# The transfers of the weight sums of a Strassen-like product: all from GpSimd, and mostly beside the first MLP product

## The chip, the core and the metric

One core of a Trainium2 chip runs the whole kernel. The metric is device time in microseconds of one execution. The engines are TensorE (PE in the profile; its weight loads are PEld), VectorE (DVE), ScalarE (ACT), GpSimd (POOL) and SyncE (SP, which only issues transfers). Transfers run on 16 DMA engines; SP, ACT and POOL each have a queue of their own to issue them from, which in the profile are q1 (SP), q10 (ACT) and q0 (POOL).

## What is computed

One layer of an encoder, on 512 tokens and 16 learned ones ahead of them, with 1024 channels, in float32:

```
h = concatenate([meta, x])
u = rmsnorm(h); proj = u @ w_in
y_rw = rwkv7_branch(...)      # a recurrence over the tokens, 8 heads
y_fx = fox_branch(...)        # attention with a forget gate, 8 heads
merged = gateA * (y_rw @ w_out_rw) + gateB * (y_fx @ w_out_fx)
h = h + merged @ w_o
z = rmsnorm(h)
h = h + square(relu(z @ w_up)) @ w_down
```

w_up is 1024 x 4096, w_down 4096 x 1024. The change is about the last line only.

## The kernel before, in words

**Split products.** Large products run on pairs of reduced-precision factors: each weight tile of 128 x 512 is loaded by SP into a buffer `wraw`, ScalarE makes its high part `whi` (a cast), VectorE or GpSimd its low part `wlo` (the difference), and TensorE does three matmuls for each product: high by high, high by low, low by high (`passes`). `load_h` (L230 to 238) does this for one tile, `load_w` for two; `wraw`, `whi` and `wlo` have four buffers each. In the front the same is done by `convert` (L442), with the low part on GpSimd (L450).

**Stages.** The front computes the projections of u, the recurrence and the attention together. Streams of work (Python generators) are woven into one another by `Turns.run` (L166), which follows a planned TensorE time, the `Clock`: a stream yields the planned time from which it may go on, and has a rank. TensorE's order is written out by it; the other engines' instructions are ordered by priority. Gate projections leave through `gt` (L489), which uses the buffers of `wraw`. Then comes the merge (L1055 to 1133): output projections with gates, where GpSimd adds the two branches (L1070), w_o, and the second norm. Then comes the MLP.

**The MLP.** Its hidden dimension is done in three slices of 4, 6 and 6 pairs of blocks (`SLICES`). In each slice the first product, w_up, is computed (L1145, 24 matmuls of 512 columns for a block of 128 hidden channels), two blocks to a pair. `up_evac` (L1148) squares what is positive into R; after the second block of a pair `left_factors` (L1154) makes seven left factors of R. R has two buffers, taken in turn. Then the second product, w_down, runs (L1235) as seven products on quarters in place of eight (Winograd's form of Strassen's scheme): (A11, B11), (A12, B21), (A22, T4), (S2, T2), (S3, T3), (S1, T1), (S4, B22), in this order. Each uses n_pairs right tiles, one for each pair, with six matmuls to a tile; `fill` (L1174) calls `load_h` for the next right tile, two tiles ahead before the product begins.

**The weight sums.** T1 to T4 are sums of quarters of w_down and are made by the DMA engines, from HBM to HBM: T1 = B11 + B12, T3 = B12 + B22, T2 = B22 + T1, T4 = B21 + T2. Each quarter is cut into eight parts c of 256 x 512 (512 KB), and each sum of each part takes a copy and then an accumulating transfer: 64 steps. Right tile j of a slice comes from part c = j // 2, so slice 0 needs c = 0 and 1, slice 1 needs 2 to 4, slice 2 needs 5 to 7. In before, `weight_sums` (L1002) is a stream of rank -1 in the front: step n waits for planned time 45 + 6 n us. Copies are issued by ScalarE (L1024), additions by GpSimd (L1022), each tied behind the last instruction of its engine that was written out until then; a copy stands about three steps ahead of its addition. The sums are loaded in the MLP by L233.

Of the kernel before, what the change touches and what calls it, by code (L numbers as in the profile page):

```python
# [9 lines left out]
F32 = mybir.dt.float32  # L10
# [4 lines left out]
ALU = mybir.AluOpType  # L15
# [12 lines left out]
CDEC = math.exp(-0.5)  # L28
SLICES = (4, 6, 6)
FIRST = (0, 4, 10)  # L30


C_MU = 0
# [155 lines left out]
def kernel(ctx, tc, ht, x, win, par, cst, gain, lora, wout, wo, wup, wdn, out, dbg=None):  # L189
    nc = tc.nc  # L190
# [3 lines left out]
    V, G, A = nc.vector, nc.gpsimd, nc.scalar  # L194
# [72 lines left out]
    gates_d = [dr.tile([128, S], F32, name=f"gd{i}") for i in range(16)]  # L267
    quarters = [[wdn[i][256 * c:256 * c + 256] for c in range(8)] for i in range(4)]
    tsum = [[dr.tile([256, 512], F32, name=f"tsum{i}") for c in range(8)] for i in range(4)]

    with ExitStack() as st:
        up = st.enter_context(tc.tile_pool(name="up", bufs=1))
# [49 lines left out]
        with tc.tile_pool(name="xp", bufs=2) as xp:  # L322
# [14 lines left out]
            for t in range(2):  # L337
# [13 lines left out]
                n = 0  # L351
# [303 lines left out]
        class Pair:  # L655
            def __init__(self, p):
                self.p, self.b0 = p, B_PAIR + 6 * p + 3
# [341 lines left out]
        turns.add(2, attention())  # L999
        turns.add(3, fox_features())  # L1000
        def weight_sums():

            def part(t, c):
                return t[c].rearrange("(a b) c -> a (b c)", b=2)

            def behind(dma, engine):
                x = next(x for x in reversed(nc.cur_bb.bb.instructions) if str(x.engine).endswith(engine) and x.name != dma.ins.name)
                tc.add_manual_dep(dma.ins, x.name, mybir.DependencyInfo(mybir.DependencyClass.NoSync, mybir.DependencyReason.DATA),
                                  reason="spread over the front")

            t1, t2, t3, t4 = tsum
            b11, b12, b22, b21 = quarters
            steps = []
            for c in range(8):
                for a, b in (((t1, b11), (t1, b12)), ((t3, b12), (t3, b22)), ((t2, b22), (t2, t1)), ((t4, b21), (t4, t2))):
                    steps += [(*a, c, False), (*b, c, True)]
            for n in range(1, len(steps) - 2, 2):
                steps[n], steps[n + 1] = steps[n + 1], steps[n]
            for n, (dst, src, c, adds) in enumerate(steps):
                yield lambda: 45.0 + 6.0 * n  # L1020
                if adds:
                    behind(nc.gpsimd.dma_start(part(dst, c), part(src, c), accum_op=ALU.add, max_dma_last_dim=2048), "Pool")  # L1022
                else:
                    behind(nc.scalar.dma_start(part(dst, c), part(src, c), max_dma_last_dim=2048), "Activation")  # L1024

        turns.add(-1, weight_sums())
        turns.add(8, projections(24 + 16))
# [20 lines left out]
    with ExitStack() as st:  # L1048
# [6 lines left out]
        for m in range(KB):  # L1055
            w = load_w(wout[m])
            pp = []
            for br in range(2):
# [4 lines left out]
                n = 0  # L1063
# [46 lines left out]
        for i in range(4):  # L1110
            po = ppo()
            n = 0
# [25 lines left out]
    with ExitStack() as st:  # L1138
        dp = st.enter_context(tc.tile_pool(name="dp", bufs=1))
# [8 lines left out]
        def up_evac(po, out):  # L1148

            r = dp.tile([128, 512], F32, name="r", bufs=2)  # L1150
            act(r, po, AF.Relu)
            V.scalar_tensor_tensor(out, po.rearrange("p (a b) -> p a b", b=256), 0.0, r.rearrange("p (a b) -> p a b", b=256), ALU.max, ALU.mult)

        def left_factors(fhi, flo, j, R):  # L1154

            def halves(a, b):
                A.copy(fhi[:, j, a:b], R[:, a:b])  # L1157
                V.tensor_tensor(flo[:, j, a:b], R[:, a:b], fhi[:, j, a:b].bitcast(F32), ALU.subtract)  # L1158

            halves(0, 3)  # L1160
            a11, a12, s1, s2, s4 = (R[:, i, :] for i in (A11, A12, S1, S2, S4))
            V.tensor_tensor(R[:, S3:S1 + 1, :], R[:, 0:3:2, :], bc(R[:, 7, :], 1, 2), ALU.subtract)
            V.tensor_tensor(s2, a11, s1, ALU.add)
            V.tensor_tensor(s4, s2, a12, ALU.subtract)  # L1164
            halves(3, 7)
# [20 lines left out]
        def soon(*jobs):  # L1186
            later.extend(jobs)

        for p0, n_pairs in zip(FIRST, SLICES):
            fhi = dp.tile([128, max(SLICES), 7, 256], F32R, name="fhi")  # L1190
            flo = dp.tile([128, max(SLICES), 7, 256], F32R, name="flo")
            blocks = list(range(2 * p0, 2 * (p0 + n_pairs)))
            held, R = [], None
            if p0 == 0:

                ws, pos = early + [load_w(wup[2])], [ppo() for i in range(3)]
                for w, po in zip(ws, pos):
                    up_part(w, po, 0, 256)
                held = list(zip(ws, pos))
            for n, b_ in enumerate(blocks):  # L1200
                if held:
                    w, po = held.pop(0)
                    up_part(w, po, 256, 512)
                else:
                    w = load_w(wup[b_])
                    po = ppo()
                    up_part(w, po, 0, 512)
                if n == 2 * n_pairs - 1:
                    fill(AHEAD)
                if n % 2 == 0:  # L1210
                    R = yp.tile([128, 8, 256], F32, name="R", tag=("y_rw", "y_fx")[n // 2 % 2])
                    up_evac(po, R[:, 0:8:7, :])
                else:
                    up_evac(po, R[:, 1:3, :])
                    left_factors(fhi, flo, n // 2, R)

            first, last = p0 == 0, p0 + n_pairs == 16

            def product(x, left, start, stop, end=False):

                for j in range(n_pairs):
                    fill(1)
                    w = ready.pop(0)
                    if later:
                        later.pop(0)()
                    if end and j >= n_pairs - 2:
                        if j == n_pairs - 2:
                            held = w
                            continue
                        order = [(i, j + d, (held, w)[d + 1]) for i in range(2) for d in (-1, 0)]  # L1230
                    else:
                        order = [(i, j, w) for i in range(2)]
                    for i, k, u in order:
                        for n, (a, c) in enumerate(passes((fhi, flo), u)):
                            mm(x[i], a[:, k, left, 128 * i:128 * i + 128], c, start=start and k == 0 and n == 0,  # L1235
                               stop=stop and k == n_pairs - 1 and n == 2)

            def own(left, end=False):
                x = [ppo() for i in range(2)]
                product(x, left, True, True, end)  # L1240
                return x

            def gathered(v, left):
                for i, x in enumerate(own(left)):
                    if first:
                        A.copy(v[:, i], x)
                    else:
                        V.tensor_tensor(v[:, i], v[:, i], x, ALU.add)

            def add(a, b, i, x, op):  # L1250
                h = hr[a][b][:, i]
                V.tensor_tensor(h, h, x, op)

            def store(a, b, i):
                r0 = 256 * a + 128 * i
                nc.sync.dma_start(out[r0:r0 + 128, 512 * b:512 * b + 512], hr[a][b][:, i])

            def added(a, b, left, op, end=False):
                for i, x in enumerate(own(left, end)):
                    add(a, b, i, x, op)  # L1260
                    if end:
                        store(a, b, i)

            gathered(v1, A11)
            added(0, 0, A12, ALU.add)
            if last:
                for i in range(2):
                    soon(lambda i=i: (add(0, 0, i, v1[:, i], ALU.add), store(0, 0, i)))
            added(1, 0, A22, ALU.add)
            product(x6, S2, first, last)  # L1270
            if last:
                for i in range(2):
                    V.tensor_tensor(v1[:, i], x6[i], v1[:, i], ALU.subtract)
                    soon(lambda i=i: add(0, 1, i, v1[:, i], ALU.add))
            product(x7, S3, first, last)
            if last:
                for i in range(2):
                    V.tensor_tensor(v1[:, i], v1[:, i], x7[i], ALU.subtract)
                    soon(lambda i=i: (add(1, 0, i, v1[:, i], ALU.subtract), store(1, 0, i)))
                for i in range(2):  # L1280
                    soon(lambda i=i: add(1, 1, i, v1[:, i], ALU.add))
            gathered(v5, S1)
            if last:
                for i in range(2):
                    soon(lambda i=i: add(0, 1, i, v5[:, i], ALU.subtract))
                for i in range(2):
                    soon(lambda i=i: (add(1, 1, i, v5[:, i], ALU.subtract), store(1, 1, i)))
            added(0, 1, S4, ALU.subtract, last)
# [77 lines left out]
```

## Time and profile before

| | |
|---|---|
| median of 3 runs | 912.88 us (911.28 to 913.75) |
| the profiled execution, its own time | 906.52 us |
| its span, first to last instruction | 904.6 us |
| granted TensorE clock, mean | 0.981 |
| bytes moved by DMA | 129.46 MB, mean 143 GB/s |

Times within the profile are microseconds from the start of the span. In a row of waits stand who waited, for whom, the total, how often, and the longest. In a row of a queue stand packets, MB and the time that the packets took, as a share of 16 engines over the stretch asked for. In a row of issues stand what was moved, the engine, how often, the size of one, and the median time from issue to landing. A row in order of time gives start, duration, engine, line and operation, and in brackets the idle time before it and what ended it.

### The profile page before, as it was taken

How to read it: one execution, taken by the hardware profiler on the slowest of the kernel's cores; microseconds unless marked ns; L12 is line 12 of the kernel's file. 1: busy time of each engine (PE TensorE's matmuls, PEld its weight loads, DVE VectorE, ACT ScalarE, POOL GpSimd, SP SyncE). 2: the span in 40 equal slices, each digit the busy share in tenths (PEclk: the TensorE clock that was granted, in tenths of full speed). 3: DMA queues.
4: the chain of work that ended last, by engine and by line, in shares of the span. 5: the costliest groups of instructions: out<-in, count | busy, mean ns of one | idle time of the engine just before them, and what ended most of it. 6: DMA issues, size and time to landing. Idle time of an engine off the chain costs nothing.

```text
span 904.6 us, 15741 instructions
## 1 busy us (share of the span) xinstructions
PE 859.2 (95%) x5896; PEld 699.9 (77%) x5896; DVE 594.3 (66%) x1168; ACT 463.6 (51%) x939; POOL 176.7 (20%) x169
## 2 busy tenths in 40 slices
PE   7789898999899899999989999999999999999998
PEld 6787785767797677677858877988888888888886
DVE  7865885546868794555476756377556675566776
ACT  7846342686355541666364544255444554354542
POOL 1063453143544353323301210000000000000000
PEclk9989999999999999999988999999999999999999
DMA  6122537656654467665685643024632367433565
GB/s 211 54 80 72 147 106 183 154 145 160 147 132 111 121 190 187 164 178 115 177 245 186 201 158 96 1 93 148 192 115 93 96 195 189 150 104 94 147 214 174
DMA packets 69771, 129.46 MB, mean 143 GB/s; under 512 B 6840, under 2 KB 7992, under 8 KB 69696
## 3 DMA queue, kind: packets, MB, share of 16 engines
q1 hardware_dynamic: 52288, 94.91, 33.4%
q0 software_dynamic: 8704, 16.78, 11.5%
q10 hardware_dynamic: 8704, 16.78, 5.7%
q8 instruction: 46, 0.75, 0.3%
q14 instruction: 29, 0.24, 0.1%
HBM read 122.13 MB, written 39.86 MB: 179 GB/s over the span
## 4 chain that ended last, share of the span: by engine, by line
PE 70%; DVE 17%; ACT 5%; DMA 4%; issue 3%; POOL 0%; POOLq 0%; SPq 0%; ACTq 0%; DVEq 0%
PE po L1145 19%; PE pj L478 15%; PE po L1235 12%; PE pd L1235 5%; PE po L1115 2%; PE po L1066 2%; PE py L627 1%; PE pw L830 1%; DMA gl<-gd 1%; DVE tmp L812 1%; DVE AX L824 1%; PE pbt L778 1%; PE psc L582 1%; DVE Tt L824 1%; DVE AX L813 1%
## 5 line engine op out<-in xcount | busy, mean ns | idle before, releaser
L237 DVE TENSOR_TENSOR wlo<-wraw,whi 128x512 fp32r<-128x512 f32 x200 | 140.4, 709 | 94.2 <-ACT whi L236 93.9
L236 ACT CAST whi<-wraw 128x512 fp32r<-128x512 f32 x200 | 123.6, 621 | 135.6 <-PE po L1145 43.3
L478 PE MATMUL pj<-uhi,whi 128*128 128x264 f32 (+1 forms) x480 | 168.9, 352 | 14.1 <-DVE okk L307 5.0
L478 PE MATMUL pj<-uhi,wlo 128*128 128x264 f32 (+1 forms) x480 | 156.8, 327 | 0.0
L478 PE MATMUL pj<-ulo,whi 128*128 128x264 f32 (+1 forms) x480 | 156.5, 326 | 0.0
L450 POOL TENSOR_TENSOR wlo<-wraw,whi 128x512 fp32r<-128x512 f32 x76 | 104.8, 1387 | 156.2 <-ACT whi L449 131.7
L478 PEld LDWEIGHTS pj<-uhi,whi 128*128 128x128 f32 x480 | 92.5, 193 | 35.7 <-issue 11.2
L478 PEld LDWEIGHTS pj<-uhi,wlo 128*128 128x128 f32 x480 | 92.8, 193 | 7.1
L478 PEld LDWEIGHTS pj<-ulo,whi 128*128 128x128 f32 x480 | 93.0, 194 | 4.3
L1145 PE MATMUL po<-zhi,whi 128*128 128x512 f32 (+1 forms) x248 | 94.8, 382 | 0.0
L1145 PE MATMUL po<-zlo,whi 128*128 128x512 f32 (+1 forms) x248 | 94.8, 382 | 0.0
L1145 PE MATMUL po<-zhi,wlo 128*128 128x512 f32 (+1 forms) x248 | 94.8, 382 | 0.0
L449 ACT CAST whi<-wraw 128x512 fp32r<-128x512 f32 x80 | 49.3, 618 | 45.2 <-PE pj L478 25.9
L1235 PE MATMUL po<-wlo,fhi 128*128 128x512 f32 x160 | 62.3, 389 | 0.0
L1235 PE MATMUL po<-whi,fhi 128*128 128x512 f32 x160 | 62.3, 389 | 0.0
L1235 PE MATMUL po<-whi,flo 128*128 128x512 f32 x160 | 62.2, 389 | 0.0
L1145 PEld LDWEIGHTS po<-zhi,wlo 128*128 128x128 f32 x248 | 46.6, 188 | 9.1
L1145 PEld LDWEIGHTS po<-zhi,whi 128*128 128x128 f32 x248 | 46.6, 188 | 9.0
L1145 PEld LDWEIGHTS po<-zlo,whi 128*128 128x128 f32 x248 | 46.6, 188 | 8.9
L1157 ACT CAST fhi<-R 128x768 fp32r<-128x768 f32 (+1 forms) x32 | 30.2, 944 | 24.0 <-DVE R L1164 13.7
L1158 DVE TENSOR_TENSOR flo<-R,fhi 128x768 fp32r<-128x768 f32 (+1 forms) x32 | 34.8, 1088 | 7.9 <-ACT fhi L1157 7.9
L1235 PEld LDWEIGHTS po<-wlo,fhi 128*128 128x128 f32 x160 | 30.0, 188 | 6.3
(294 smaller groups left out, 1657.5 us busy)
## 6 DMA issues: line engine op xcount, KB each, us to landing
wraw<-in_win SPq DMA_DIRECT2D x84, 256.0 KB, 3.2
tsum<-in_wdn ACTq DMA_DIRECT2D x32, 512.0 KB, 4.5
wraw<-in_wup SPq DMA_DIRECT2D x64, 256.0 KB, 2.6
wraw<-tsum SPq DMA_DIRECT2D x64, 256.0 KB, 2.9
wraw<-in_wdn SPq DMA_DIRECT2D x48, 256.0 KB, 2.7
tsum<-in_wdn POOLq DMA_DIRECT2D x16, 512.0 KB, 7.2
tsum<-tsum POOLq DMA_DIRECT2D x16, 512.0 KB, 6.1
gd<-gt SPq DMA_DIRECT2D x16, 256.0 KB, 2.5
```

The costliest lines, as they stand in the source:

```text
L236: A.copy(hi, raw)
L237: low.tensor_tensor(lo, raw, hi.bitcast(F32), ALU.subtract)
L449: A.copy(hi, raw)
L450: low.tensor_tensor(lo, raw, hi.bitcast(F32), ALU.subtract)
L478: mm(po, a, b[:, k, a0:a1], start=n == 0, stop=n == 23)
L824: V.tensor_copy(dst[rs_, :, o:o + 32], src[rs_, :, :n2].rearrange("p t n -> p n t"))
L1066: mm(po, a, b[:, k, :], start=n == 0, stop=n == 11)
L1115: mm(po, a[:, k, 128 * i:128 * i + 128], b[:, k, :], start=n == 0, stop=n == 23)
L1145: mm(po[:, t0:t1], a, b[:, k, t0:t1], start=n == 0, stop=n == 23)
L1157: A.copy(fhi[:, j, a:b], R[:, a:b])
L1158: V.tensor_tensor(flo[:, j, a:b], R[:, a:b], fhi[:, j, a:b].bitcast(F32), ALU.subtract)
L1235: mm(x[i], a[:, k, left, 128 * i:128 * i + 128], c, start=start and k == 0 and n == 0, stop=stop and k == n_pairs - 1 and n == 2)
```

## The change

The sums become a small class with a list of the 64 steps and a method that issues the next one. Every transfer is issued by GpSimd, copies too, tied behind GpSimd's last instruction. The order is by rounds: the four copies of part 0 first, and from then on the four additions of part c alternate with the four copies of part c + 1, so that some eight steps lie between a copy and its addition. T4's addition stands two steps behind the one of T2 that it reads. The front issues 12 steps (`HEAD`), at planned times 50 + 380 / 12 n us. In the MLP, after the evacuation of the second block of a pair, GpSimd copies one column of R into a tile `pace`, and four steps are issued behind it: 52 steps in the first 13 of the 16 pairs. Nothing else changes.

```
+HEAD = 12
...
+    class Sums:
+        def __init__(self):
+            t1, t2, t3, t4 = tsum
+            b11, b12, b22, b21 = quarters
+            rounds = []
+            for c in range(8):
+                rounds.append([(t[c], b[c], False) for t, b in ((t1, b11), (t3, b12), (t2, b22), (t4, b21))])
+                rounds.append([(t[c], b[c], True) for t, b in ((t1, b12), (t3, b22), (t2, t1), (t4, t2))])
+            self.steps = rounds[0]
+            for a, b in zip(rounds[1::2], rounds[2::2] + [[]]):
+                for n in range(4):
+                    self.steps += a[n:n + 1] + b[n:n + 1]
+
+        def step(self):
+            if not self.steps:
+                return
+            dst, src, adds = self.steps.pop(0)
+            dst, src = (t.rearrange("(a b) c -> a (b c)", b=2) for t in (dst, src))
+            prev = next((x for x in reversed(nc.cur_bb.bb.instructions) if str(x.engine).endswith("Pool")), None)
+            dma = G.dma_start(dst, src, max_dma_last_dim=2048, **({"accum_op": ALU.add} if adds else {}))
+            if prev is not None:
+                tc.add_manual_dep(dma.ins, prev.name, mybir.DependencyInfo(mybir.DependencyClass.NoSync, mybir.DependencyReason.DATA),
+                                  reason="spread over the kernel")
...
         def weight_sums():
-            ...
-            for n, (dst, src, c, adds) in enumerate(steps):
-                yield lambda: 45.0 + 6.0 * n
-                if adds:
-                    behind(nc.gpsimd.dma_start(part(dst, c), part(src, c), accum_op=ALU.add, max_dma_last_dim=2048), "Pool")
-                else:
-                    behind(nc.scalar.dma_start(part(dst, c), part(src, c), max_dma_last_dim=2048), "Activation")
+            for n in range(HEAD):
+                yield lambda: 50.0 + 380.0 / HEAD * n
+                sums.step()
...
                     up_evac(po, R[:, 1:3, :])
+                    if sums.steps:
+                        G.tensor_copy(dp.tile([128, 1], F32, name="pace"), R[:, 2, :1])
+                        for _ in range(4):
+                            sums.step()
                     left_factors(fhi, flo, n // 2, R)
```

More of the change, by code (lines that the diff above doesn't have):

```diff
@@ L269 @@
     tsum = [[dr.tile([256, 512], F32, name=f"tsum{i}") for c in range(8)] for i in range(4)]
+    class Sums:
[20 more added lines that the diff above has]
+                                  reason="spread over the kernel")
+    sums = Sums()
     with ExitStack() as st:
@@ L1001, in weight_sums @@
         def weight_sums():
[L1003 to L1018, printed above, removed]
-            for n, (dst, src, c, adds) in enumerate(steps):
-                yield lambda: 45.0 + 6.0 * n
-                if adds:
-                    behind(nc.gpsimd.dma_start(part(dst, c), part(src, c), accum_op=ALU.add, max_dma_last_dim=2048), "Pool")
-                else:
-                    behind(nc.scalar.dma_start(part(dst, c), part(src, c), max_dma_last_dim=2048), "Activation")
+            for n in range(HEAD):
+                yield lambda: 50.0 + 380.0 / HEAD * n
+                sums.step()
         turns.add(-1, weight_sums())
```

## The prediction

> **What bounds the kernel now.** I read the page first, then busy time by stage, then the waits of TensorE and GpSimd, and last the transfers and the conversions of the second MLP product.
>
> The page's busy times and the shares of the chain that ended last:
>
> ```profile
> PE 859.2 (95%) x5896; PEld 699.9 (77%) x5896; DVE 594.3 (66%) x1168; ACT 463.6 (51%) x939; POOL 176.7 (20%) x169
> PE 70%; DVE 17%; ACT 5%; DMA 4%; issue 3%; POOL 0%; POOLq 0%; SPq 0%; ACTq 0%; DVEq 0%
> ```
>
> TensorE sets the end, GpSimd is on the chain for 0%. Where TensorE is idle is seen by stage (columns: PE busy with count, PEld, DVE, ACT, POOL, granted clock, DMA share, GB/s):
>
> ```profile
> 45.00:480.00 435.00, 405.64 (x3739) 321.75 (x3739) 287.10 (x674) 227.16 (x540) 160.57 (x147) 0.96 0.57 148
> 570.00:618.00 48.00, 47.89 (x284) 42.60 (x283) 26.52 (x40) 19.14 (x32) 0.00 (x0) 1.00 0.19 59
> 618.00:656.00 38.00, 38.00 (x170) 31.46 (x169) 25.22 (x39) 21.20 (x36) 0.00 (x0) 1.00 0.61 184
> 656.00:721.00 65.00, 65.00 (x289) 53.83 (x287) 41.07 (x62) 29.31 (x45) 0.00 (x0) 1.00 0.33 102
> 721.00:778.00 57.00, 57.00 (x253) 47.23 (x252) 36.64 (x56) 28.36 (x45) 0.00 (x0) 1.00 0.65 188
> ```
>
> The front (45 to 480) has 29.4 us of idle TensorE. The MLP has none: 570 to 618 and 656 to 721 are first products (up), 618 to 656 and 721 to 778 second products (down), each slice up then down. So the change can win only in the front and lose only in the MLP. What the front's TensorE waits for:
>
> ```profile
> PE psr L763 <- DVE L L767: 5.6, 5, 2.2
> PE pj L478 <- DVE okk L307: 5.0, 1, 5.0
> PE pj L478 <- DVE orr L307: 3.9, 2, 2.0
> PE pj L478 <- ACT gt L489: 3.8, 1, 3.8
> ```
>
> Three of the four are VectorE work that no weight sum touches.
>
> **What leaves the front.** The operations of the sums, and the waits of GpSimd for them:
>
> ```profile
> L233 SPq DMA_DIRECT2D wraw<-tsum x64: 319/320/660, 621.0 to 883.3; - x64
> L1024 ACTq DMA_DIRECT2D tsum<-in_wdn x32: 497/498/589, 82.1 to 455.8; - x32
> L1022 POOL DMA_DIRECT2D tsum<-in_wdn x16: 859/880/1197, 91.1 to 444.0; - x16
> L1022 POOL DMA_DIRECT2D tsum<-tsum x16: 870/878/972, 118.2 to 460.4; - x16
> POOL tsum L1022 <- DMA tsum<-in_wdn: 34.5, 5, 9.9
> POOL tsum L1022 <- DMA tsum<-tsum: 6.3, 1, 6.3
> ```
>
> ScalarE loses 32 issues of 0.498 us, 15.9 us. GpSimd goes in the front from 32 issues of 0.88 us (28.2 us) to 12 (10.6 us): eight copies and the four additions of c = 0. Its 40.8 us of waits go too, since with eight steps of 32 us planned time no source is young. With GpSimd at 0% of the chain, none of that counts by itself: behind the waiting GpSimd stood the low parts of projection weights (L450), and TensorE has no wait for them among its first rows. What is late next is the same VectorE work. What can count is where a transfer or an issue is on the chain:
>
> ```profile
> 141.71 2.65 DMA wraw<-in_win
> 145.16 0.95 POOL wlo L450
> 146.12 3.94 DMA wraw<-in_win
> 410.80 0.50 ACTq L1024
> ```
>
> In the up product of slice 1, without sums beside it, a weight load lands sooner:
>
> ```profile
> wraw<-in_wup SPq DMA_DIRECT2D x18, 256.0 KB, 2.5
> ```
>
> So 2.65 + 3.94 - 2 x 2.5 = 1.6 us, and the 0.5 us issue: 2.1 us gained. The bounds: nothing, if VectorE is late there anyway, and 4.3 us, the whole 3.8 us wait for the gate evacuation (L489, whose buffer is one of the four of the loads) and the 0.5. I take 2.1, the nearest rows. The order of ScalarE's and GpSimd's other work may shift when the issues leave; no row prices it, and I give it 2 us either way, an estimate from the spread of the single waits above (2.0 to 2.2 us). The last addition of before is issued at 460.4 and the merge begins near 477, so "none in the merge" changes nothing.
>
> **What comes into the MLP.** GpSimd is empty there (0.00 in the rows), so 13 pace copies and 52 issues have room: 4 x 0.88 = 3.5 us in each pair of blocks. The rows of two pairs' evacuations, then a GpSimd instruction with almost no elements:
>
> ```profile
> 667.84 0.68 DVE L1152 SCALAR_TENSOR_TENSOR R<-po,r 128x512 f32<-128x512 f32 x1
> 678.76 0.68 DVE L1152 SCALAR_TENSOR_TENSOR R<-po,r 128x512 f32<-128x512 f32 x1
> 173.86 0.13 POOL L643 MEMSET orr<- 128x48 f32 x1
> ```
>
> A pair lasts 10.9 us. The pace copy should cost about 0.13 us (bounds: nothing and the 0.88 us of an issue); it waits for R, and behind it on GpSimd stand only the four transfers. The one added wait that is long is t4's addition, which needs t2's, two steps earlier in the same pair: about the 6 to 7 us of a landing, with the next pair's copy behind it and nobody else. The writer of R that waits for the pace copy comes two pairs later. The sums of c = 1 are issued by the second pair (near 598), the first load of a sum at 621.0; c = 4 is issued by the eighth pair, near 700, and TensorE wants its first T4 tile, the 17th of slice 1's down product, at 721.2 + 16 x 1.36 = 742.9. Those costs I set at nothing; if that cover goes, the loads queue on SP behind a late sum.
>
> What isn't free is the DMA engines. The page's queues, and then two stretches of 4 us in the front in which additions and loads ran together (the queues' shares are of the 4 us; the last column of an issue is us to landing). First the page:
>
> ```profile
> q0 software_dynamic: 8704, 16.78, 11.5%
> q10 hardware_dynamic: 8704, 16.78, 5.7%
> ```
>
> An addition takes 0.115 x 904.6 / 32 = 3.25 us of all 16 engines, a copy 1.61 us. A pair's two and two take 9.7 us. From 242 to 246, and the loads of 200 to 204 and of 208 to 212:
>
> ```profile
> q0 software_dynamic: 197, 0.37, 53.3%
> q1 hardware_dynamic: 246, 0.45, 43.2%
> wraw<-in_win SPq DMA_DIRECT2D x1, 256.0 KB, 5.3
> ...
> wraw<-in_win SPq DMA_DIRECT2D x1, 256.0 KB, 4.5
> ...
> wraw<-in_win SPq DMA_DIRECT2D x2, 256.0 KB, 6.5
> ```
>
> Beside additions a load lands after 4.5 to 6.5, mean 5.4 us. Does the MLP have cover for that? In the up product two loads serve 5.44 us. With four raw buffers, a load is issued when the tile four earlier is converted (ScalarE 0.62 + VectorE 0.69, with issue about 1.36), so one tile comes every (landing + 1.36) / 4. At 5.4 that is 1.69 us, under the 2.72 needed: no loss. The down product uses a tile every 1.36 us, and the rule allows a landing of 4.1 us. Its rows, TensorE's from the chain and ScalarE's eleventh conversion, of slice 0 and of slice 1:
>
> ```profile
> 617.80 16.32 PE po L1235 x72
> 628.89 0.62 ACT L236 CAST whi<-wraw 128x512 fp32r<-128x512 f32 x1 [0.91 <-DMA wraw<-tsum]
> ...
> 721.16 24.48 PE po L1235 x108
> 733.80 1.29 ACT L236 CAST whi<-wraw 128x512 fp32r<-128x512 f32 x2 [2.46 <-DMA wraw<-in_wdn]
> ```
>
> 72 matmuls in 16.32 us are 1.36 us for a tile's six. In slice 0 the eleventh tile is wanted at 617.80 + 13.6 = 631.4 and ready at 628.89 + 0.62 + 0.69 = 630.2: 1.2 us of slack. In slice 1 it is wanted at 734.8 and ready at 735.1: the slack is used up already in before, behind the left factors. The fourth pair's and the tenth pair's steps are released by the last evacuation before the down product, so they run beside exactly these loads. A batch of 9.7 us, at the 53% that additions held above, lasts 18.2 us: 10.8 tiles, each late by 1.69 - 1.36 = 0.33 us, 3.6 us. Slice 0: 3.6 - 1.2 = 2.4 us. Slice 1: 3.6 us. Slice 2's last steps are its third pair's, 33 us before its down product: nothing. The MLP loses 6.0 us. Bounds: nothing, if loads land within 4.1 us, and the 12.7 us of the backlog below.
>
> **The sum.** -2.1 + 6.0 = +3.9 us. The profiled execution took 906.52 us (span 904.6), so 910.4; the median of the runs is 912.88, 6.4 above it, and there it is 916.8.
>
> A rule that speaks against the change: the Trainium skill, "DMA: Bandwidth & Descriptors", section "Queues, rings and completion order", says that each DMA engine goes round its queues packet by packet. The trace leans that way: 246 packets of loads beside 197 of additions. What it would make of the time is a rival below.
>
> **The rivals.**
> First, **the relief of the front alone**: the loads of the down product still land within 4.1 us, because no more than one addition is in flight (t4's waits for t2's to land), and the front gives back all 4.3 us: 902.2, on the median 908.6, faster. For it: DMA had 0.65 at most in the MLP and TensorE did not notice. Against: the zero slack of slice 1. It decides at a landing of 4.1 us.
> Second, **loads bound by the share of the engines, not by landing**: at equal packets a load gets what an addition gets, 0.37 to 0.45 MB in 4 us, so a tile of 0.262 MB takes 2.6 us. An addition of 0.524 MB lasts 5.7 us there; two last 11.4, in which 11.4 x (2.6 - 1.36) / 2.6 = 5.4 us are lost; two transitions less 1.2 give 9.6, net +7.5: 920.4. That is what the page's rule would give here. Against it: from four loads in flight more packets may be taken than from one.
> Third, **a backlog**: the up product needs 9.7 + 0.33 x 10.9 = 13.3 us of engines in a pair of 10.9, 2.4 too many. After six pairs 14 us are left over in slice 1 and some 4 in slice 0: 23.7 / 0.53 = 45 us and 26 us of contention, 8.8 and 5.1 - 1.2 = 3.9 us lost; net +10.6: 923.5. Packet times overlap, which speaks against it.
> Fourth, **the change moves work that nobody feels**, as far as it does what it says: slice 0 keeps its cover, slice 1 loses about what the front gains (2.1): 912.9, no change.
>
> **How the numbers follow.** The forecast has 0.37, the first rival 0.29, the second 0.12, the third 0.07, the fourth 0.15. No change means within 0.3% (2.7 us), about what a measurement of this kernel can tell: faster 0.29, same 0.15, slower 0.56. The range reaches from the first rival, with 1.6 for the scatter of the runs (911.28 to 913.75) and part of the 2 us of reordering, 907, to the third, 924.
>
> **What would show it.** Right: TensorE idle beginning some 10 us after the start of the down products of slices 0 and 1, and none in slice 2; conversions there waiting for DMA for more than 0.91 and 2.46 us; weight loads landing above 4.1 us beside the sums; the front shorter by about 2 us, with no GpSimd wait for a sum. Wrong: down products of 38 and 57 us as before (first rival), or conversions late in the up products as well (third). A front that changes by more than 4 us either way would say that I priced it from the wrong rows, and sums not landed when SP comes to load them would void the costs that I set at nothing.

## The result, and the profile after

| | before | after |
|---|---|---|
| median, 12 runs each | 912.15 us (907.14 to 914.89) | 912.42 us (908.28 to 919.38) |
| profiled execution, its own time | 906.52 us | 911.76 us |
| its span | 904.6 us | 910.0 us |
| granted clock, mean | 0.981 | 0.979 |

The ratio after to before is 1.0008, 95% interval 0.9988 to 1.0028: no change, where a slowdown to 916.8 us had been forecast. Note the first profile of before: 906.52 us lies below all 12 of the other runs. It was an unusually quick execution, and that matters below.

The page of after, busy times and the shares of the chain that ended last:

```profile
PE 865.3 (95%) x5896; PEld 701.3 (77%) x5896; DVE 591.3 (65%) x1168; ACT 465.0 (51%) x939; POOL 203.2 (22%) x214
PE 68%; DVE 16%; DMA 7%; ACT 5%; issue 3%; POOL 0%; SPq 0%; ACTq 0%; DVEq 0%; POOLq 0%
```

DMA went from 4% to 7% of the chain. Where it entered is seen by stage (columns: PE busy, PEld, DVE, ACT, POOL, clock, DMA share, GB/s; up, down of slice 0, up, down of slice 1, up of slice 2):

```profile
570.00:614.00 44.00, 43.89 (x259) 38.99 (x258) 24.65 (x37) 17.63 (x29) 10.54 (x15) 1.00 0.64 170
614.00:656.00 42.00, 40.13 (x168) 30.87 (x167) 24.81 (x38) 21.21 (x35) 3.49 (x5) 1.00 0.86 255
656.00:721.00 65.00, 65.00 (x288) 53.82 (x287) 41.38 (x63) 29.41 (x45) 17.35 (x25) 1.00 0.89 238
721.00:783.00 62.00, 60.13 (x254) 48.10 (x253) 36.66 (x56) 28.24 (x45) 3.50 (x5) 0.97 0.81 233
783.00:849.00 66.00, 66.00 (x293) 54.68 (x292) 41.70 (x63) 29.78 (x46) 11.21 (x15) 1.00 0.78 199
```

The up product of slice 1 has a DMA share of 0.89 and no idle TensorE; only the two down products lose. Their part of the chain of after, in order of time:

```profile
568.28 2.87 PE po L1154 x24
...
612.45 7.12 DMA wraw<-in_wdn
621.04 6.50 DMA wraw<-tsum
629.01 6.13 DMA wraw<-tsum
645.31 10.88 PE po L1248 x48
656.19 65.07 PE po L1154 x287
726.43 6.59 DMA wraw<-in_wdn
734.49 6.38 DMA wraw<-tsum
...
783.50 65.28 PE po L1154 x288
```

This is one buffer going round: a load of 7.12 us, a cast and a difference, and the next load into it at 621.04, 8.59 us after the one before. Four such buffers give a tile every 2.15 us, then (629.01 - 621.04 = 7.97) every 1.99 us. TensorE wants one every 1.36. The chain shows the loads that were late, not the average one; the queues and issues from 614 to 640 (q0 GpSimd, q1 SP; packets, MB, share; last column of an issue: median us to landing):

```profile
q0 software_dynamic: 1307, 3.32, 50.7%
q1 hardware_dynamic: 2079, 3.79, 42.2%
...
wraw<-tsum SPq DMA_DIRECT2D x14, 256.0 KB, 5.0
```

So the median of fourteen loads is 5.0 us, in a stretch that includes some 5 us after the batch had landed. ScalarE's conversions fall behind in the same place; in the brackets is what they waited for:

```profile
619.67 0.62 ACT L237 CAST whi<-wraw 128x512 fp32r<-128x512 f32 x1 [1.57 <-DMA wraw<-in_wdn]
...
627.64 0.62 ACT L237 CAST whi<-wraw 128x512 fp32r<-128x512 f32 x1 [1.33 <-DMA wraw<-tsum]
...
635.25 1.30 ACT L237 CAST whi<-wraw 128x512 fp32r<-128x512 f32 x2 [4.20 <-DMA wraw<-tsum]
```

The four transfers issued at the end of slice 0's up product (the batch) run beside these loads. On GpSimd:

```profile
615.88 0.64 POOL L1225 COPY pace<-R 128x1 f32<-128x1 f32 x1 [7.35 <-DVE R L1161]
616.46 0.88 POOL L293 DMA_DIRECT2D tsum<-tsum  x1
617.03 0.87 POOL L293 DMA_DIRECT2D tsum<-in_wdn  x1
626.58 0.89 POOL L293 DMA_DIRECT2D tsum<-tsum  x1 [8.68 <-DMA tsum<-tsum]
627.16 0.89 POOL L293 DMA_DIRECT2D tsum<-in_wdn  x1
```

So four landmarks say where each profiled execution gained or lost: the start of the up product in each slice, and the end. They are read from the chains (the first row of each up product), and all twelve experiments are in the table too. A span belongs to one profiled execution and a median to all runs of a kernel, so they need not have the same order:

| kernel | up, slice 0 | slice 0 lasts | slice 1 lasts | span | median (ratio to before, 95% interval) |
|---|---|---|---|---|---|
| before, first profile | 572.13 | 83.75 | 122.40 | 904.6 | |
| after | 568.28 | 87.91 | 127.31 | 910.0 | 912.42 (0.9988 to 1.0028) |
| before again | 577.80 | 83.73 | 122.40 | 910.8 | 912.70 (0.9963 to 1.0014) |
| no sums | 570.77 | 83.74 | 122.40 | 903.9 | 903.28 (0.986 to 0.992) |
| all 64 in the front | 582.17 | 83.74 | 122.39 | 915.1 | 914.48 (0.9989 to 1.0037) |
| none after a slice's last pair | 569.59 | 84.51 | 122.43 | 905.2 | 906.88 (0.9907 to 0.9966) |
| 24 in the front | 570.53 | 83.74 | 122.40 | 903.6 | 909.74 (0.9942 to 0.9995) |
| after, seven raw buffers | 569.45 | 83.74 | 122.40 | 901.9 | 900.74 (0.9836 to 0.9899) |
| plain traffic from ScalarE | 584.92 | 83.74 | 122.40 | 918.1 | 920.71 (1.006 to 1.0117) |
| thin transfers | 571.62 | 83.82 | 122.40 | 904.9 | 904.29 (0.9881 to 0.9938) |
| additions eight pairs behind | 574.04 | 83.75 | 122.40 | 908.3 | 908.74 (0.9935 to 0.9993) |
| before, seven raw buffers | 573.97 | 83.74 | 122.40 | 906.7 | 911.22 (0.9967 to 1.002) |
| seven buffers, none after last pair | 576.83 | 83.75 | 122.39 | 909.3 | 902.50 (0.9897 to 0.9957) |
| traffic without waits | 578.57 | 83.74 | 122.40 | 911.2 | 913.03 (0.9964 to 1.0013) |

Slices 0 and 1 take the same time to 0.1 us in every kernel without sums at their ends; in after slice 0 takes 4.2 us and slice 1 4.9 us more, 9.1 together. From the start of slice 2 to the end all have 126.3 to 127.1 us, but for the kernel without steps after a slice's last pair (128.7) and the one with additions eight pairs behind (128.1). What lies ahead of slice 0 scatters by several us from profile to profile, so it is judged by the medians: with 9.1 us lost in the MLP and 0.3 in all, the front of after gave back about 8.8.

### The profile page after: what moved, and what is told of

It is laid out like the page before. It is cut to its first block, busy times and chain, and to the rows that moved or that the text cites. A ratio compares the mean times of both kernels' runs of the same rounds, so it can differ in the third digit from the quotient of the medians.

```text
span 910.0 us, 15777 instructions
## 1 busy us (share of the span) xinstructions
PE 865.3 (95%) x5896; PEld 701.3 (77%) x5896; DVE 591.3 (65%) x1168; ACT 465.0 (51%) x939; POOL 203.2 (22%) x214
## 4 chain that ended last, share of the span: by engine, by line
PE 68%; DVE 16%; DMA 7%; ACT 5%; issue 3%; POOL 0%; SPq 0%; ACTq 0%; DVEq 0%; POOLq 0%
PE po L1154 19%; PE pj L507 18%; PE po L1248 8%; PE pd L1248 4%; PE po L1124 2%; DMA wraw<-tsum 2%; PE po L1075 2%; PE pw L859 2%; DMA wraw<-in_wdn 2%; PE psc L611 1%; DVE wlo L238 1%; PE py L656 1%; DVE tmp L841 1%; DMA wraw<-in_wup 1%; DVE AX L853 1%
## 5 line engine op out<-in xcount | busy, mean ns | idle before, releaser
L1225 POOL COPY pace<-R 128x1 f32<-128x1 f32 x13 | 8.0, 614 | 213.8 <-DVE R L1161 213.8
```

## The experiments

Theory after the result (theory A in the expectations): both terms of the sum are real and larger than forecast, about 9 us each, and cancel. Rival (theory B): the front gives only 3 to 4 us (the profiles' 572.13 to 568.28), and the rest is scatter.

**Before again**, no edit.

> The kernel before, unchanged, for a second profile and for the scatter. Theory A (both terms are real and cancel: the front of before is usually longer than in its first profile, which was the quickest of all its runs): span near 910, and the extra 5 us over the first profile lie ahead of the MLP, whose products end as before with no idle TensorE (38 and 57 us down products). Theory B (the front gives back only the 3 to 4 us that the two first profiles show, and the MLP's loss of 9 us in the profile of after is what a profile does, not what a run does): span near 905 again. Ratio to before 1.000 in both, as a null.

Measured: 912.70 us, up product of slice 0 at 577.80. The first profile was 5.7 of its 6.2 us early by then: from 45 us to that start TensorE is idle for 31.0 us in the first profile and for 34.1 in this one, and the other 2.6 us are busy time, at a mean clock of 0.97 in the first and 0.96 in this one. One stretch shows it, before's first profile, then this one, columns as above:

```profile
284.00:304.00 20.00, 17.55 (x123) 13.47 (x124) 15.37 (x31) 11.03 (x21) 8.69 (x7) 1.00 0.49 134
```

```profile
284.00:304.00 20.00, 17.55 (x114) 13.47 (x110) 14.07 (x28) 11.17 (x21) 8.57 (x7) 0.91 0.50 130
```

The same busy and idle time, but a clock of 0.91 instead of 1.00. And at the entrance of the merge transfers stand on the chain of this profile, where the first had none:

```profile
460.33 4.67 DMA gd<-gt
465.03 4.29 DMA wraw<-in_wout
```

**No sums.**

```
-        turns.add(-1, weight_sums())
...
-        B11, B22, B21, T1, T2, T3, T4 = quarters[0], quarters[2], quarters[3], *tsum
+        B11, B22, B21, T1, T2, T3, T4 = quarters[0], quarters[2], quarters[3], *([quarters[1]] * 4)
```

> The 64 transfers of the sums are left out, and the products that would read T1 to T4 read a plain quarter of w_down instead (same loads, same matmuls). It is the floor: neither the front nor the MLP has the sums beside it. Theory A: 8 to 9 us under before (ratio 0.990 to 0.991), all of it ahead of the MLP; a front that ends near 470 and an MLP as in before. Theory B: 3 to 4 us under before (0.996).

Measured: 903.28 us, 8.7 below the 911.95 of before in the same comparison. Slices 0 and 1 are as in before, so that is the whole price of 64 sums in the front; the forecast had 2.1 for taking most of them out.

**All 64 in the front, from GpSimd.**

```
-HEAD = 12
+HEAD = 64
```

> The changed kernel with all 64 steps in the front (HEAD = 64), so nothing is beside the MLP: the new order and GpSimd as the only issuer, alone. Theory A with the DMA engines as the front's cost: about as before (1.000), since the front carries the same bytes. Rival, the waits of GpSimd and the copies' issues on ScalarE were the front's cost: as fast as without sums, 4 to 9 us under before. Second rival, GpSimd's 64 issues of 0.88 us hurt more than they help: 3 us or more over before.

Measured: 914.48 us, as before (ratio 1.0013), and the MLP untouched. One issuing engine and eight steps of distance change nothing that these runs can tell; where the transfers run does.

**No steps after a slice's last pair.**

```
-                    if sums.steps:
+                    if sums.steps and n < 2 * n_pairs - 1:
```

> The changed kernel, but no steps at the last pair of a slice, so that no batch is released right at the start of a down product; the steps come one pair later where skipped. If the batch at the transition is what the loads of the down product are late behind (my term of 2.4 and 3.6 us): the 9 us of the two transitions go nearly to nothing, 6 to 9 us under after. If a backlog of the earlier pairs is the larger part (third rival): only about half comes back, 3 to 5 us under after.

Measured: 906.88 us; slice 0 loses 0.8 us and slice 1 nothing. The batches at the transitions made 8.3 of the 9.1 us, and no backlog is carried from the up product (the third rival of the prediction). The time came down by 5.5 us and not by 6 to 9: the steps pushed back now reach slice 2, whose down product has a load of a sum of 5.31 us on its chain at 853.43, and which takes 2.2 us longer to the end than in after (128.7 against 126.5).

**24 in the front, none after the last two pairs.**

```
-HEAD = 12
+HEAD = 24
...
-                    if sums.steps:
+                    if sums.steps and n < 2 * n_pairs - 3:
```

> The changed kernel with 24 of its 64 steps in the front instead of 12, and no steps after the last two pairs of blocks of a slice; all sums are computed. If the transitions are the whole loss in the MLP and 12 steps more in the front cost little, as long as no sum is waited for there: 905 to 908 us, with up products and down products as long as before the change, like the version without steps at the last pair of a slice (906.9). If each step in the front costs its share of what 64 steps cost there (about 9 us for 64, 1.7 for 12 more): 908 to 909 us.

Measured: 909.74 us against 912.34, with an MLP as long as in before. That is nearer to the second answer, and somewhat above it: steps in the front cost, even though GpSimd has no wait for a sum ahead of the MLP in this profile. The price isn't proportional to the number of steps: by the medians 24 steps cost 6.5 us over no sums at all, 64 cost 9, and 12 hardly anything (the next run has them). What makes the second twelve so dear was not tried.

**Seven raw buffers.**

```
...
-                ready.append(load_h(right[j // 2][128 * (j % 2):128 * (j % 2) + 128], V, "w", (4, 4, 4)))
+                ready.append(load_h(right[j // 2][128 * (j % 2):128 * (j % 2) + 128], V, "w", (4, 4, 4), dp if len(line) % 2 else None))
```

With a pool given, `load_h` takes its raw tile from a ring of three there. Every second tile does, so the ring of three bounds both: it is as if there were six buffers.

> The changed kernel with seven buffers instead of four for the raw weight tiles of the down products (every second tile has a ring of three of its own); all sums are computed, with the steps at the same places as in the change. If the loss at the two transitions comes from landing time over buffers (6.5 us of landing + 1.36, over 4, is 1.97 us for a tile; over 6 it is 1.31, under the 1.36 needed): slice 0 and slice 1 lose under 1.5 us each instead of 4.2 and 4.9, the time is 904 to 907 us, and loads beside the additions still land after some 6.5 us. If it is the share of the DMA engines: tiles still come only every 2 us or later while the additions run, loads then take 9 us and more to land with six in flight, only the three tiles more of lead help, and the slices lose 2 to 4 us each: 908 to 911 us.

Measured: 900.74 us, faster than the 904 to 907 expected and the lowest median of all, and slices of 83.74 and 122.40 us. It lies even below the kernel without sums (903.28), which was to be the floor; the intervals of the two ratios overlap (0.9836 to 0.9899, 0.986 to 0.992), and nothing here explains a real difference. The queues and issues of this kernel from 614 to 640, beside the batch (as above for after):

```profile
q0 software_dynamic: 1432, 3.72, 53.8%
q1 hardware_dynamic: 2589, 4.72, 49.8%
...
wraw<-tsum SPq DMA_DIRECT2D x7, 256.0 KB, 6.6
draw<-tsum SPq DMA_DIRECT2D x7, 256.0 KB, 6.2
```

A load still takes 6.2 to 6.6 us, and it does not matter: (6.6 + 1.36) / 6 = 1.33 us a tile. With more loads in flight the loads moved more in the same 26 us (4.72 MB beside 3.72 MB of sums, where after had 3.79 beside 3.32). The second rival's equal shares are refuted: with no more than 3.72 MB in 26 us a tile of 0.262 MB would have come every 1.83 us. The Trainium skill, "DMA: Bandwidth & Descriptors", section "Queues, rings and completion order", has the engines go round the queues packet by packet; these counts, 2589 against 1432, show that this was no even split here. Whether both queues had work all the time, which an even split would need, is not shown.

**Plain traffic from ScalarE, and thin transfers.** In the first, 48 plain copies of 1 MB take the place of the sums; in the second the sums move a sixteenth of the bytes.

```
...
+            for n in range(48):
+                yield lambda: 45.0 + 8.0 * n
+                dst = dr.tile([512, 512], F32, name=f"sink{n}")
+                src = wdn[n % 4][512 * (n // 4 % 4):512 * (n // 4 % 4) + 512]
...
```

> The kernel before, with its 64 weight sums replaced by 48 plain copies of 1 MB from DRAM to DRAM, all issued by ScalarE at the same spacing over the front: about the same time of the DMA engines as the sums, but nothing issued and nothing waited for by GpSimd. The sums are left out: the four factors that need them are read from one plain quarter of the weights. If the front's cost of the sums is their DMA traffic beside the weight loads: 909 to 912 us, as with the sums. If it is what GpSimd's issues and waits do to its other work and to VectorE: 903 to 905 us, as with no sums (903.3), and the stretch from the first state copy to the last key block stays at 83 us instead of 89.

```
-                return t[c].rearrange("(a b) c -> a (b c)", b=2)
+                return t[c][:, :32]
```

> The kernel before with the same 64 transfers, issued by the same engines at the same places and with the same waits between them, but each only 32 of the 512 columns wide: a sixteenth of the bytes. Nearly all of the sums is left out, and the four factors that need them are read from one plain quarter of the weights. If the front's cost of the sums is DMA traffic: 903 to 905 us. If it is the issues and waits on GpSimd: 908 to 912 us, the stretch from the first state copy to the last key block near 89 us; if only the waits count and not the issues, 904 to 907 with GpSimd's waits for sums under 10 us instead of 40.8.

Measured: 920.71 and 904.29 us. Traffic alone, with nothing issued by GpSimd, costs 8 us more than the sums. The sums' issues without most of their bytes cost 1.0 us over no sums, less than the intervals, although GpSimd still waited 18.3 us for copies. The front's price is the traffic. Loads issued from 170 to 255, in before's first profile, then in thin (last column: median us to landing):

```profile
wraw<-in_win SPq DMA_DIRECT2D x12, 256.0 KB, 4.7
```

```profile
wraw<-in_win SPq DMA_DIRECT2D x12, 256.0 KB, 3.1
```

In after they take 2.6 us. I had expected 909 to 912 for the plain copies. In that kernel the loads of this stretch take only 2.9 us, so its loss has to lie elsewhere: from 45 to 570 its loads of `in_win` have a median of 3.8 us (3.2 in before, 2.7 in thin) and its stores of gates 5.1 us (2.5 and 2.1). Why 1 MB copies do more harm than as much engine time of sums was not tried.

**Additions eight pairs behind.** To tell apart how the bytes act: through GpSimd, which waits 34.5 us for copies in before while the low parts queue behind, or through the loads.

```
...
-            for n in range(1, len(steps) - 2, 2):
-                steps[n], steps[n + 1] = steps[n + 1], steps[n]
+            for i in range(32 + 8):
+                steps += copies[i:i + 1] + (adds_[i - 8:i - 7] if i >= 8 else [])
```

> The kernel before with the same 64 transfers in the front, copies from ScalarE and additions from GpSimd as there, but each addition eight pairs of steps behind its copy instead of one or two; all sums are computed. The bytes beside the front's weight loads stay (loads near 5 us to land between 170 and 255 us), the waits of GpSimd for a copy go (from 34 to 37 us to under 5). If the front's cost is GpSimd waiting, with the low parts behind it that then run late and beside VectorE's urgent work: 904 to 906 us. If it is the loads that land late beside the transfers: 909 to 912 us, the stretch from the first state copy to the last key block near 89 us.

Measured: 908.74 us, between the two answers, and the edit did not do what it was for: GpSimd still waited 19.1 us for copies and 16.9 us for other sums. It decides nothing.

**Traffic without waits.**

```
-                    behind(nc.gpsimd.dma_start(part(dst, c), part(src, c), accum_op=ALU.add, max_dma_last_dim=2048), "Pool")
+                    sink = dr.tile([512, 512], F32, name=f"sink{n}").rearrange("(a b) c -> a (b c)", b=4)
+                    whole = wdn[n % 4][512 * (c % 4):512 * (c % 4) + 512].rearrange("(a b) c -> a (b c)", b=4)
+                    behind(nc.gpsimd.dma_start(sink, whole, max_dma_last_dim=2048), "Pool")
```

> The kernel before, in which each of the 32 accumulating transfers of GpSimd is a plain copy of 1 MB to a place of its own (about the same time of the DMA engines, 3.2 us each); ScalarE's 32 copies, the order and the spacing stay, but no transfer depends on another, so GpSimd waits for none. The additions are left out: the four factors that need sums are read from one plain quarter of the weights. If the front's cost is the bytes beside the weight loads, which then land late (4 us and more between 170 and 255 us): 909 to 914 us. If it is GpSimd's 34 to 37 us of waits for copies, with the low parts of the projection weights behind them: 903 to 906 us, whatever the loads take to land.

Measured: 913.03 us, ratio 0.9989. GpSimd waits for none of these transfers in this profile, and nothing is gained. Its loads from 170 to 255, and its queues there:

```profile
q0 software_dynamic: 2448, 9.44, 31.2%
...
wraw<-in_win SPq DMA_DIRECT2D x12, 256.0 KB, 4.1
```

So GpSimd's waits alone aren't the price: without them nothing was gained here, and in thin 18.3 us of them cost nothing that can be measured. A part of the price they could still be, for the copies of 1 MB that stand here for the additions did more harm than sums in the run before. Traffic on the DMA engines is the price, and the loads that land late beside it are the part of it that the profiles show on the chain. Which late load costs how much was not settled: the loss is spread (next section).

**Seven buffers in before; seven buffers and no last batches.** The edits are those of the run with seven buffers, in the kernel before, and of that run and the one without steps after a slice's last pair together.

> The kernel before with seven raw buffers for the down products' tiles as in the run of the change with seven; all sums are computed, in the front as before. If the buffers matter only because sums run beside the loads there: no change, 911 to 913 us, up products and down products as before. If they have a gain of their own (the last down product, which has two short waits for loads): 908 to 911 us.

Measured: 911.22 us, ratio 0.9994 (0.9967 to 1.002): the buffers show no gain of their own.

> The changed kernel with seven raw buffers and, besides, no steps after the last pair of a slice; all sums are computed. If seven buffers cover the additions at the transitions whole: 900 to 902 us, as with seven buffers alone. If something of the loss was left there: 897 to 899 us.

Measured: 902.50 us, ratio 0.9927 (0.9897 to 0.9957), beside 0.9868 (0.9836 to 0.9899) with the batches. Taking the batches away adds nothing to the buffers, where 897 to 899 us would have said that it does. Both are about 1% under before and after; their intervals overlap, and these runs can't choose between them.

## Why the prediction was wrong, point by point

**The front, -2.1 us: the step that failed.** Measured, taking all sums out is -8.7 us (no sums), thinning them -8.0 (904.29 against 912.34), and the change itself gave back about 8.8 there. The prediction put the term together from two loads and an issue on one chain, and bounded it by one 3.8 us wait; that bound of 4.3 us, too, is half of what was measured. Three things went wrong:

- The profile it argued from was an unusually quick one: between 284 and 304, and at the merge's entrance, it had escaped what the second profile of the same kernel paid. The stretch into the merge, in before again and in after:

```profile
440.00:480.00 40.00, 34.20 (x197) 24.66 (x195) 21.81 (x70) 19.60 (x53) 6.23 (x7) 0.85 0.78 204
```

```profile
440.00:480.00 40.00, 36.18 (x203) 25.72 (x202) 23.95 (x71) 22.11 (x57) 2.71 (x3) 0.91 0.44 149
```

  A DMA share of 0.78 falls to 0.44 and TensorE is busy 2 us longer. The clock, 0.06 higher here, does not go with the bytes: without any sums it is 0.87 in this stretch. The prediction had dismissed the merge because the last addition is issued at 460.4 and the merge begins near 477; but the loads of the merge's weights are issued from 449.94 on in the same profile, beside the last sums, and in before again one of them is on the chain (465.03).
- It read the front's loss off whom TensorE waited for (VectorE, mostly) and concluded that the sums don't matter there. The name of the last to come says nothing of what made it late. From 170 to 255, before again has 76.98 us of busy TensorE at a DMA share of 0.64, after 81.03 at 0.27, thin 80.99 at 0.25, and the kernel whose GpSimd waits for no transfer 77.20 at 0.63: 4 us that go with the traffic, although most of the waits there are for VectorE. By which steps a late load reaches VectorE was only argued, through the low parts on GpSimd, and stays open.
- It looked for the loss in single waits, and the loss is spread. From 45 us to the start of slice 0's up product TensorE is idle for 31.0 and 34.1 us in the two profiles of before, 25.0 without sums, 27.2 in thin and 26.4 in after: 4 to 9 us of idle time, while the mean clock over this stretch is 0.96 or 0.97 in all five. So in these profiles the price of the sums in the front is idle TensorE, and not the clock (last section).

The 0.5 us for ScalarE's issue is too small for these runs: thin keeps all 32 issues and is 1.0 us above no sums, within the intervals.

**The MLP, +6.0 us: right place, right mechanism, undersized.** The loss is in the down products of slices 0 and 1, none in slice 2 and none in an up product (the rows of after), it is released by the last pair's evacuation, and it goes when the batch goes or when there are more raw buffers: each shown by a run. The size: 4.2 + 4.9 = 9.1 us, half as much again as the forecast 6.0. The mis-sized term is the landing of loads beside additions, 5.4 us from the front's rows (a mean over three rows; by loads, one row being two, it is 5.7). In after, the loads that were waited for took 6.1 to 7.1 us. With 6.6 the same working gives (6.6 + 1.36) / 4 = 1.99 us a tile, 0.63 late, 9.1 tiles in 18.2 us, 5.8 a transition and 4.6 + 5.8 = 10.4. That is somewhat too much, and the more so as some 1.7 of slice 1's 4.9 us are clock, which the working doesn't have (last section).

**Set at nothing, and rightly so:** t4's wait for t2 (8.68 us in the batch above, 6 to 7 forecast, nobody behind it that TensorE waits for), SP's order (in the profile of after SP never waits for an unfinished sum), the up products at a DMA share of 0.89. The pace copy took 0.64 us, not 0.13; nothing felt it.

**The rivals.** The fourth gave the right time, 912.9, from 2.1 us on each side; the runs show 9 on each side. It was right in that the sides cancel, its prices were wrong by a factor of four, and slice 0, which was to keep its cover, lost 4.2 us: the right time was luck. The first was wrong about landing and the third about a backlog. The second had 9.6 us for the MLP, nearest to the 9.1, but by equal shares, which the run with seven buffers refutes: luck as well.

**The test that was set.** "A front that changes by more than 4 us either way would say that I priced it from the wrong rows": no sums changed it by 8.7.

## What to carry to other kernels

Before taking transfers as free because their issuing engine isn't on the chain, look at what loads beside them take to land, and divide landing plus conversion by the number of buffers. Here that period (1.99 us with four buffers, 1.33 with six) against the consumer's 1.36 decided, in the stage where the consumer is fastest. A transfer moved out of one busy place into another can bring nothing although both effects are large; run each half alone. And a forecast that leans on one profile should ask first how that execution stands among the runs.

## What the runs showed of the hardware

**After a stall of TensorE the clock can be lower for a while.** Before's first profile, then after, TensorE busy and clock in 5 us each:

```profile
240.00:245.00 5.00, 2.79 (x31) 2.32 (x30) 4.92 (x10) 1.41 (x3) 4.35 (x5) 1.00 0.94 194
245.00:250.00 5.00, 3.88 (x20) 3.22 (x22) 4.93 (x11) 0.00 (x0) 0.00 (x0) 0.52 1.12 226
```

```profile
740.00:745.00 5.00, 3.38 (x10) 2.29 (x9) 3.36 (x6) 2.48 (x4) 0.00 (x0) 0.78 0.65 220
745.00:750.00 5.00, 5.00 (x20) 4.02 (x20) 2.50 (x4) 2.32 (x4) 0.00 (x0) 0.88 0.72 204
```

In the first pair 2.2 us of idle in 5 are followed by a clock of 0.52. In the second, 1.6 us of idle go with 0.78 and then 0.88: 5 x 0.22 + 5 x 0.12 = 1.7 us of full speed are missing there, in slice 1's down product. In slice 0's, with as much idle in sum (1.87 us in each), the clock stayed at 1.00. It is not the idle time alone that decides: from 240 to 250, after and the kernel without sums have the same 3.44 us and then 5.00 of busy TensorE, and the clock differs (after first):

```profile
240.00:245.00 5.00, 3.44 (x31) 2.86 (x28) 4.95 (x11) 0.63 (x1) 1.24 (x1) 0.94 0.30 105
245.00:250.00 5.00, 5.00 (x40) 4.32 (x39) 4.73 (x13) 3.13 (x6) 0.48 (x1) 0.72 0.00 0
```

```profile
240.00:245.00 5.00, 3.44 (x38) 2.83 (x39) 4.89 (x11) 1.63 (x3) 2.52 (x2) 1.00 0.31 108
245.00:250.00 5.00, 5.00 (x52) 4.42 (x49) 4.91 (x12) 2.81 (x6) 0.47 (x1) 1.00 0.00 0
```

The Trainium skill, "TensorE: Matmul & The Clock Gate", section "What's actually happening", has a window of about 3.4 us that runs freely, after which an idle array falls to half its clock. These rows agree with it in part. No single wait here fills such a window: the longest are 2.19 us in the first pair (with 1.12 us more soon after it) and 1.39 in the second. But a window whose phase isn't the kernel's would make the same stall cost one run some us and the next none, and the times of one kernel do go with their mean clock (of the twelve runs with additions eight pairs behind, the fastest has 903.93 us at 0.987, the slowest 913.80 at 0.971). That this is the cause of the scatter was not tested.
